# A gated attention layer on one core: queries, keys and gates projected transposed over 512 tokens, and an earlier layer norm

## The chip, the cores and the metric

The kernel runs on one core of a Trainium2 chip. The core has TensorE (PE in the rows: matmuls, and PEld: its weight loads), VectorE (DVE), ScalarE (ACT), GpSimd (POOL), and SyncE (SP), which issues the DMA transfers here. Each engine takes its instructions in order; engines wait for each other through semaphores. The metric is the device time of one execution in microseconds, as the median of several runs.

## The reference, cut to what matters

A layer norm over x (2048 tokens, 1024 features) is followed by one projection, whose 7592 columns are cut into queries, keys, values and gates of three branches. Branch A attends to the 256 keys that an index score selects, B is a differential attention with 4 heads of two softmaxes, C attends to 256 memory tokens. Each branch output is multiplied by silu of its gate, projected, weighted with a sigmoid gate, and the sum is projected and normalized.

```python
h = _layer_norm(x, ln_in_g, ln_in_b)
proj = h @ w_in[l]
(a_q, a_k, a_v, a_gate, i_q, i_k, i_w, b_q, b_k, b_v, b_gate,
 c_q, c_gate, m_gate) = _split_cols(proj, IN_SPLITS)
a_q = _partial_rope(a_q.reshape(bsz, seq, A_HEADS, A_HEAD_DIM), pos)
...
o_a = _dsa_attention(a_q, a_k, a_v, i_q, i_k, i_w).reshape(bsz, seq, A_WIDTH)
y_a = (o_a * jax.nn.silu(a_gate)) @ w_proj_a[l]
...
y_b = (o_b.reshape(bsz, seq, B_WIDTH) * jax.nn.silu(b_gate)) @ w_proj_b[l]
y_c = (o_c.reshape(bsz, seq, C_WIDTH) * jax.nn.silu(c_gate)) @ w_proj_c[l]
g = jax.nn.sigmoid(m_gate.reshape(bsz, seq, N_BRANCH, D_MODEL))
merged = g[:, :, 0] * y_a + g[:, :, 1] * y_b + g[:, :, 2] * y_c
h = _layer_norm(DEEPNORM_ALPHA * h + merged @ w_out[l], ln_g[l], ln_b[l])
```

`_partial_rope` rotates the first 16 of a head's 64 features (two halves of 8) by an angle that depends on the token.

## The kernel before, in words

Every fp32 matrix product is done with operands split into a high and a low part (`split`, L62 to L69: a copy, and a subtraction that leaves the rest), and three matmuls (`mm3`, L71 to L74). Tokens come in 16 blocks of 128; `hP` holds the split, transposed h for pairs of blocks, 256 tokens, and half of the blocks (8) is resident at a time.

The program has four stages. (1) For each half of the tokens: the layer norm and transposition (`prologue`, L187), the jobs `dense_ai` (queries of A in two jobs `aq`, then the index job `dense_ai01`: A's key and value, index queries, keys and weights), the search for the 256 best keys of each token (`topk_group`; VectorE and ScalarE count scores above a threshold bit by bit, L520, L529, L533), and `dense_b` (`bk`, `bv`, `bq`). For blocks 8 to 15 x is loaded and normalized only behind `dense_b(0)`. (2) B attention (from L647): logits `lg` (L623, L624), a copy to `P` with a running minimum (L633, L637), exp on ScalarE (L691), the two softmaxes combined (L697), transpositions `pt` (L703), their split `pr`, and the product with the values `ops` (L709), then a normalization (L712 to L724) and a store to `ob_d` (L725). (3) A attention (from L731) with the branches B and C projected beside it. (4) The branch A, the output projection `fz` and the last layer norm. The gate jobs `dense_g` (`cq`: C's queries, `sg`: silu gates, `tm`: sigmoid gates; 20 jobs per half) depend on h alone and can stand anywhere; they stand between other matmuls as filler.

A dense job (`dense`, L244) loads 256 columns of weights (`load_win`, `wr` raw, `w` split; the subtraction on GpSimd, the copy on ScalarE early on and on GpSimd later) and runs over 4 pairs of blocks into the PSUM tile `dps`. For `aq`, `bk`, `bv`, `bq` and the silu gates of A and B, h is the stationary operand and 256 weight columns move, so the output has tokens on partitions. For `cq`, `tm` and the gate of C the weights are stationary and 256 tokens move. The heads then go through `emit`: a copy to `do`, rope on GpSimd (L133 to L136), and `heads_out` (L212): a split of each 128-token block into `dt` on VectorE, four transpositions on TensorE (L223, into `dpt` or `psT`), a copy to `de` on ScalarE, and a store to DRAM. B and A attention load heads from DRAM again (`kg`, `bq`, `KA`, `aq`).

The order of the instructions on each engine is not written by hand: a list scheduler with a model of durations takes them from the program's order and its priorities (`tc.high_priority` raises those of `emit`), and each engine then runs its list in order. The pools with their numbers of buffers bound how far it can go ahead.

## Time and profile before

| | us |
|---|---|
| median of 3 runs | 2969.26 |
| lowest and highest run | 2966.13 and 2979.38 |
| the profiled execution's span | 2965.9 |
| TensorE busy in it | 2830.5 |
| VectorE busy | 2279.2 |
| ScalarE busy | 1442.6 |
| GpSimd busy | 983.2 |

The span of the profiled execution is what the rows below add up to. A busy time is the union of an engine's instructions; TensorE's matmuls overlap in the pipeline, so that a duration of one is longer than the distance between two starts. "Idle before" is the time in which an engine had nothing, and behind the arrow stands what released it.

### The profile page before, as it was taken

Reading aid. Unit: us, or ns where it says so; the run is one execution under the profiler, and the core shown is the slowest. Engines: PE = TensorE matmul, PEld = TensorE weight load, DVE = VectorE, ACT = ScalarE, POOL = GpSimd, SP = SyncE. Lnnn points to the kernel's source line nnn. Section 1 sums busy time; section 2 is a strip of 40 time slices with the busy share of each in tenths; the row PEclk is TensorE's granted clock in tenths of the full one; section 3 lists DMA queues with packets and bytes.
Section 4 is the critical chain, followed back from the end, with each engine's and each line's share of the span. In section 5 each row is a group of like instructions: output and inputs, shape, how many; then the busy total and the mean of one; then the engine's idle time right before and its main releaser. Section 6 shows DMA issues by size and latency. Waiting matters only on the chain. (4 is left out here: it accounts for less than half of the span.)

```text
span 2965.9 us, 57460 instructions
## 1 busy us (share of the span) xinstructions
PE 2830.5 (95%) x21616; PEld 2715.7 (92%) x21616; DVE 2279.2 (77%) x5309; ACT 1442.6 (49%) x2806; POOL 983.2 (33%) x1064
## 2 busy tenths in 40 slices
PE   7979998999999998999999999999999999988998
PEld 6979998999999998999999999988999999978887
DVE  6499988999899998676667766658787777776655
ACT  4345673677266772333344334446566556544100
POOL 6663547242522236323324222302222222200221
PEclk9999999999999999999999999999999999999999
DMA  6554434433232234624234242273433333256532
GB/s 208 171 191 138 159 113 156 133 119 114 94 101 76 82 93 147 201 73 140 89 118 142 77 128 80 75 242 110 133 114 119 102 113 102 86 172 224 172 131 79
DMA packets 320949, 379.47 MB, mean 128 GB/s; under 512 B 26400, under 2 KB 236832, under 8 KB 320160
## 3 DMA queue, kind: packets, MB, share of 16 engines
q1 hardware_dynamic: 320672, 375.80, 40.2%
q8 instruction: 171, 2.80, 0.4%
q14 instruction: 106, 0.87, 0.1%
HBM read 236.02 MB, written 139.69 MB: 127 GB/s over the span
## 5 line engine op out<-in xcount | busy, mean ns | idle before, releaser
L72 PE MATMUL dps<-hP,w 128*128 128x256 f32 x2048 | 582.6, 284 | 15.1 <-DVE do L69 9.9
L74 PE MATMUL dps<-hP,w 128*128 128x256 f32 x2048 | 581.7, 284 | 0.0
L73 PE MATMUL dps<-hP,w 128*128 128x256 f32 x2048 | 581.2, 284 | 0.0
L72 PE MATMUL dps<-w,hP 128*128 128x256 f32 (+1 forms) x1664 | 491.1, 296 | 12.5 <-POOL w L64 3.1
L73 PE MATMUL dps<-w,hP 128*128 128x256 f32 (+1 forms) x1664 | 490.0, 295 | 0.0
L74 PE MATMUL dps<-w,hP 128*128 128x256 f32 (+1 forms) x1664 | 487.9, 294 | 0.0
L72 PEld LDWEIGHTS dps<-hP,w 128*128 128x128 f32 x2048 | 392.6, 192 | 21.6 <-DVE do L69 10.7
L74 PEld LDWEIGHTS dps<-hP,w 128*128 128x128 f32 x2048 | 392.5, 192 | 4.4 <-POOL w L69 0.3
L73 PEld LDWEIGHTS dps<-hP,w 128*128 128x128 f32 x2048 | 392.7, 192 | 3.6
L533 ACT ACTIVATE ja<-sall,thr 128x1280 bf16<-128x1280 f32 (+4 forms) x224 | 302.2, 1349 | 122.6 <-DVE thr L529 107.1
L64 POOL TENSOR_SCALAR w<-wr 128x1024 fp32r<-128x1024 f32 x120 | 135.5, 1129 | 629.5 <-PE dps L74 404.9
L72 PEld LDWEIGHTS dps<-w,hP 128*128 128x128 f32 x1664 | 324.0, 195 | 16.8 <-issue 4.3
L69 POOL TENSOR_TENSOR w<-wr,w 128x1024 fp32r<-128x1024 f32 (+1 forms) x128 | 332.1, 2595 | 15.0 <-ACT w L66 6.9
L520 DVE TENSOR_SCALAR_CACHE_REDUCE jd<-sall,thr 128x1408 bf16<-128x1408 f32 (+6 forms) x231 | 330.9, 1433 | 5.9
L73 PEld LDWEIGHTS dps<-w,hP 128*128 128x128 f32 x1664 | 324.3, 195 | 1.8
L74 PEld LDWEIGHTS dps<-w,hP 128*128 128x128 f32 x1664 | 323.8, 195 | 2.2
L691 ACT ACTIVATE P<-P,nm 128x128 f32<-128x128 f32 (+15 forms) x128 | 154.1, 1204 | 197.8 <-DVE nm L690 187.5
L626 DVE CUSTOM_DVE_ANT_0 AP<-lg,bias 128x512 f32<-128x512 f32 (+3 forms) x304 | 181.9, 619 | 68.4 <-PE lg L624 25.1
L66 ACT CAST apr<-apt 128x512 fp32r<-128x512 f32 (+1 forms) x288 | 158.4, 563 | 141.7 <-PE apt L777 108.4
L633 DVE TENSOR_SCALAR_CACHE_REDUCE P<-lg 128x512 f32<-128x512 f32 (+3 forms) x288 | 170.4, 596 | 72.3 <-PE lg L624 71.2
L493 DVE SCALAR_TENSOR_TENSOR sall<-ir,iw,sall 128x512 f32<-128x512 f32 (+3 forms) x266 | 217.1, 865 | 8.9 <-ACT ir L489 8.0
L782 PE MATMUL aops<-apr,VA 128*128 128x256 f32 x1088 | 206.7, 297 | 16.8 <-DVE apr L69 6.7
(249 smaller groups left out, 7109.2 us busy)
## 6 DMA issues: line engine op xcount, KB each, us to landing
wr<-in_w_in_dram SPq DMA_DIRECT2D x112, 512.0 KB, 3.9
tm_d<-do SPq DMA_DIRECT2D x96, 256.0 KB, 2.1
bq<-qb_d SPq DMA_DIRECT2D x128, 128.0 KB, 3.1
aq<-qa_d SPq DMA_DIRECT2D x128, 128.0 KB, 3.1
yt<-tm_d SPq DMA_DIRECT2D x64, 256.0 KB, 3.6
sg_d<-do SPq DMA_DIRECT2D x48, 256.0 KB, 2.1
ys<-sg_d SPq DMA_DIRECT2D x48, 256.0 KB, 3.1
facc<-mg_d SPq DMA_DIRECT2D x48, 256.0 KB, 4.1
```

The source lines that it names most:

```text
L66: A.copy(H, src)
L69: el.tensor_tensor(L, src, H.bitcast(F32), op=ALU.subtract)
L72: PE.matmul(ps, lH, rH, start=start, stop=False)
L73: PE.matmul(ps, lH, rL, start=False, stop=False)
L74: PE.matmul(ps, lL, rH, start=False, stop=stop)
L493: V.scalar_tensor_tensor(s[:, c0:c0 + cn], r[:, :cn], iw[:, h:h + 1], s[:, c0:c0 + cn], op0=ALU.mult, op1=ALU.add)
L520: V.tensor_scalar(jd[:, :L], sc[b], t.bitcast(F32)[:, i:i + 1], None, op0=op, op1=ALU.add, accum_out=dst[:, i:i + 1])
L533: A.activation(ja[:, :L], sc[b], AF.Sign, bias=thr.bitcast(F32)[:, i:i + 1], scale=-1.0, accum_out=cnt[:, i:i + 1])
L626: V.tensor_tensor_reduce(P[:, c0:c0 + cn], ps[:, :cn], bias[:, c0:c0 + cn], scale=-0.125, scalar=-LOW, op0=ALU.add, op1=ALU.min, accum_out ...
L633: V.tensor_scalar(P[:, c0:c0 + n0], ps[:, :n0], -0.125, None, op0=ALU.mult, op1=ALU.min, accum_out=mx[:, col, nch:nch + 1])
L691: A.activation(p[:, :L], p[:, :L], AF.Exp, bias=nm[:, c:c + 1], scale=-1.0, accum_out=sm[:, c:c + 1])
L782: PE.matmul(o_ps.rearrange("p a d -> p (a d)"), VA[:, k0 + i], pr[:, a, i].rearrange("p e q -> p (e q)"), start=(k0 + i == 0 and a == 0), ...
```

## The change

All dense jobs except `bv` and the index job now have weights as the stationary operand and 512 tokens as the moving one, in `hQ` tiles of four blocks (the very first `aq` job still goes by 256). For `aq`, `bq`, `bk` the columns of a job's weights are put in another order while they are split (four strips of 32 columns, that hold the 8 features of a rope half for 4 heads, and then 128), so that rope on the transposed tile is three operations on 64 partitions, with a table `rope_t` that is loaded for each tile; the split of the result is on GpSimd, and nothing is transposed afterwards. `bv`'s split goes to GpSimd behind a copy on ScalarE. The silu gates of A and B are stored transposed, and `gated` multiplies after the transposition of the attention output instead of before. The layer norm of blocks 8 to 15 comes right behind `dense_ai(0)`; its result is stored to `h_d` and loaded again by `prologue` as `hx`. The input pool `xp` has 5 buffers instead of 8. The blocks of the second half's top-k groups are [8, 9, 14, 15] and [10, 11, 12, 13]. DRAM tiles hold 512 tokens. Over the program there are 4896 matmuls of 512 columns and 960 of 256 in place of 10752 of 256 into `dps`, 144 transpositions at the old L223 in place of 528, and 32 casts and 32 subtractions into `dt` in place of 128 each.

```diff
+        if len(src.shape) > len(H.shape):
+            H, L = (x.rearrange("p k (h d) -> p k h d", d=src.shape[-1]) for x in (H, L))
...
-    qa_d = [[dram(f"qa_d{j}_{p}", [4, 128, 256]) for p in range(NP)] for j in range(2)]
+    qa_d = [dram(f"qa_d{q}", [8, 128, 512]) for q in range(NQ)]
...
+            hQ[b // 4] = hTp.tile([128, 2, KT, 512], F32R, name=f"hQ{b // 4}", tag=f"hQ{b // 4 % 2}")
...
-    xp = pool("xp", 8, side="right")
+    xp = pool("xp", 5, side="right")
...
+    def normalize(b):
         xt = xin[b]
         mu, rs = norm_stats(p1, xt)
-        if b < 8:
-            nb = p1.tile([128, 1], F32, name="nb")
-            G.tensor_scalar(nb, mu, rs, -1.0, op0=ALU.mult, op1=ALU.mult)
-            A.activation(xt, xt, AF.Identity, bias=nb, scale=rs)
-        else:
-            V.tensor_scalar(xt, xt, mu, rs, op0=ALU.subtract, op1=ALU.mult)
+        nb = p1.tile([128, 1], F32, name="nb")
+        G.tensor_scalar(nb, mu, rs, -1.0, op0=ALU.mult, op1=ALU.mult)
+        A.activation(xt, xt, AF.Identity, bias=nb, scale=rs)
         (V if b < GV else G).tensor_tensor(xt, xt, gin, op=ALU.mult)
         V.tensor_tensor(xt, xt, bin_, op=ALU.add)
         SP.dma_start(h_d[b], xt)
+
+    def prologue(b, banks):
+        if b < 8:
+            normalize(b)
+            xt = xin[b]
+        else:
+            xt = dp.tile([128, D], F32, name="hx", bufs=3)
+            SP.dma_start(xt, h_d[b])
         to_hT(hT_tile(b), xt, banks)
...
+            H, L = (w[:, a, 4 * i:4 * i + 4, :n] for a in range(2))
+            if not heads:
+                split(H, L, raw, eh, el)
+                continue
+            rh = raw.rearrange("p k (h d) -> p k h d", d=64)
+            for u in range(4):
+                o = slice(32 * u, 32 * u + 32)
+                split(H[:, :, o], L[:, :, o], rh[:, :, :, 8 * u:8 * u + 8], eh, el)
+            split(H[:, :, 128:256], L[:, :, 128:256], rh[:, :, :, 32:64], eh, el)
...
+    def dense(kind, half, cols, idx, w=None, step=512):
         n = sum(c for _, c in cols)
         if w is None:
-            w = load_win(cols, A if early[0] else G)
-        for p in range(4 * half, 4 * half + 4):
-            ps = dqs.tile([128, 2, 256], F32, name="dps")
-            for i in range(2):
-                if kind in ("cq", "tm") or (kind == "sg" and idx[0] == 2):
-                    c = slice(i * 128, (i + 1) * 128)
-                    h = hP[p]
+            w = load_win(cols, A if early[0] else G, heads=kind in ("aq", "bq", "bk"))
+        if kind == "bv":
+            for p in range(4 * half, 4 * half + 4):
+                ps = dqs.tile([128, 2, 256], F32, name="dps")
+                for i in range(2):
+                    h = hT[2 * p + i]
                     for k in range(KT):
-                        mm3(ps[:, i], w[:, 0, k, c], w[:, 1, k, c], h[:, 0, k], h[:, 1, k], k == 0, k == KT - 1)
-                    continue
-                h = hT[2 * p + i]
-                for k in range(KT):
-                    mm3(ps[:, i, :n], h[:, 0, k], h[:, 1, k], w[:, 0, k, :n], w[:, 1, k, :n], k == 0, k == KT - 1)
+                        mm3(ps[:, i, :n], h[:, 0, k], h[:, 1, k], w[:, 0, k, :n], w[:, 1, k, :n], k == 0, k == KT - 1)
+                with tc.high_priority():
+                    emit(kind, idx, p, ps, n)
+            return
+        for g in range(2):
+            def col(a, k):
+                return w[:, a, k, 128 * g:128 * g + 128]
+            for q in range(2 * half, 2 * half + 2):
+                ps = dqs.tile([128, 512], F32, name="dps")
+                for c0 in range(0, 512, step):
+                    c = slice(c0, c0 + step)
+                    for k in range(KT):
+                        mm3(ps[:, c], col(0, k), col(1, k), hQ[q][:, 0, k, c], hQ[q][:, 1, k, c], k == 0, k == KT - 1)
+                with tc.high_priority():
+                    emit_t(kind, idx, g, q, ps)
+
+    def emit_t(kind, idx, g, q, ps):
+        if kind in ("sg", "tm"):
+            r, j = idx
+            o = dw.tile([128, 512], F32, name="do", bufs=3)
             with tc.high_priority():
-                emit(kind, idx, p, ps, n)
+                A.activation(o, ps, AF.Tanh, scale=0.5)
+                if kind == "sg":
+                    V.scalar_tensor_tensor(o, o, 1.0, ps, op0=ALU.add, op1=ALU.mult)
+            SP.dma_start((sg_d if kind == "sg" else tm_d)[r][q][:, 2 * j + g], o)
+            return
+        if kind == "cq":
+            e = [dw.tile([128, 512], F32R, name="do", bufs=3) for _ in range(2)]
+            with tc.high_priority():
+                split(e[0], e[1], ps, A, V)
+            for a in range(2):
+                SP.dma_start(cq_d[q][:, 2 * idx + g, a], e[a].bitcast(F32))
+            return
+        e = dp.tile([128, 2, 512], F32R, name="de")
+        dst = {"aq": qa_d, "bq": qb_d, "bk": kb_d}[kind][q].rearrange("h (a d) t -> h a d t", a=2)[4 * idx:4 * idx + 4]
+        if g:
+            o = dw.tile([128, 512], F32, name="do", bufs=3)
+            with tc.high_priority():
+                A.copy(o, ps)
+            split(e[:, 0], e[:, 1], o, G, G)
+            for a in range(2):
+                SP.dma_start(dst[:, a, 32:64], e.bitcast(F32)[:, a])
+            return
+        o = dw.tile([128, 512], F32, name="do", bufs=3)
+        sw = dp.tile([64, 512], F32, name="rsw", bufs=1)
+        with tc.high_priority():
+            A.copy(o, ps)
+            A.copy(sw[0:32], ps[32:64])
+            A.copy(sw[32:64], ps[0:32])
+        rq = dp.tile([64, 2, 512], F32, name="rq", bufs=1)
+        for i in range(2):
+            src = rope_t[i, :, :, 512 * q:512 * q + 512]
+            SP.dma_start(rq[32 * i:32 * i + 32], src[None].to_broadcast([4, 8, 2, 512]))
+        last_rope[0] = G.tensor_tensor(sw, sw, rq[:, 1], op=ALU.mult).ins
+        G.tensor_tensor(o[0:64], o[0:64], rq[:, 0], op=ALU.mult)
+        G.tensor_tensor(o[0:64], o[0:64], sw, op=ALU.add)
+        split(e[:, 0], e[:, 1], o, G, G)
+        for a in range(2):
+            for u in range(4):
+                SP.dma_start(dst[:, a, 8 * u:8 * u + 8], e.bitcast(F32)[32 * u:32 * u + 32, a])
...
         if kind == "bv":
             v = dp.tile([128, 2, 2, 2, 128], F32R, name="de")
+            o = dw.tile([128, 2, 256], F32, name="do", bufs=3)
             with tc.high_priority():
-                for i in range(2):
-                    pv = ps[:, i].rearrange("p (h d) -> p h d", d=128)
-                    split(v[:, :, i, 0], v[:, :, i, 1], pv, A, V)
+                A.copy(o, ps)
+            for i in range(2):
+                split(v[:, :, i, 0], v[:, :, i, 1], o[:, i].rearrange("p (h d) -> p h d", d=128), G, G)
...
+            dense("aq", half, [(C_AQ + 256 * j, 256)], j, W0 if first else None, 256 if first else 512)
...
+    for b in range(8, NB):
+        load_x(b, xp)
+        normalize(b)
...
+    topk_group([8, 9, 14, 15])
+    topk_group([10, 11, 12, 13])
...
+    def gated(pool, psp, pname, o, s, r, b, oT):
         t = slice(128 * (b % 2), 128 * (b % 2) + 128)
-        SP.dma_start(s, sg_d[r][b // 2][b % 2])
-        eng.tensor_tensor(o, o, s, op=ALU.mult)
+        SP.dma_start(s, sg_d[r][b // 4][:, :, 128 * (b % 4):128 * (b % 4) + 128])
         ps = psp.tile([128, 4, 128], F32, name=pname, bufs=2 if pname == "cps" else 1)
         for c in range(4):
             PE.transpose(ps[:, c], o[:, c * 128:(c + 1) * 128], idf)
         with tc.high_priority():
-            A.activation(oT[:, 0, :, t], ps, AF.Copy, scale=0.5)
-            V.scalar_tensor_tensor(oT[:, 1, :, t], ps, 0.5, oT[:, 0, :, t].bitcast(F32), op0=ALU.mult, op1=ALU.subtract)
+            V.scalar_tensor_tensor(s, ps, 0.5, s, op0=ALU.mult, op1=ALU.mult)
+            A.copy(oT[:, 0, :, t], s)
+            G.tensor_tensor(oT[:, 1, :, t], s, oT[:, 0, :, t].bitcast(F32), op=ALU.subtract)
```

The lists of the engines change with it. TensorE, the end of B attention, before (`lg<-KA` are A's first logits, `dps` a gate job):

```order
L72 MATMUL dps<-hP_25620,w 128x256
L73 MATMUL dps<-hP_25620,w 128x256
L623 MATMUL lg<-KA_15284,aq 128x512 x2
L74 MATMUL dps<-hP_25620,w 128x256
L72 MATMUL dps<-hP_25620,w 128x256
...
L624 MATMUL lg<-KA_15284,aq 128x512 x2
L73 MATMUL dps<-hP_25620,w 128x256
```

A's first logits stand among the last gate matmuls. TensorE, the last gate matmul, after (`pt`, `lg<-kg`, `ops` are B's):

```order
L76 MATMUL dps<-hQ_22199,w 128x512
L77 MATMUL dps<-hQ_22199,w 128x512
L745 MATMUL pt<-idf,P 128x128 x8
L667 MATMUL lg<-kg,bq 128x512
L668 MATMUL lg<-kg,bq 128x512
...
L751 MATMUL ops<-vg,pr 128x256
...
L751 MATMUL ops<-vg,pr 128x256 x8
L745 MATMUL pt<-idf,P 128x128 x3
L751 MATMUL ops<-vg,pr 128x256 x7
```

Behind this there are no more `dps` in the list: 434 of 1088 `ops`, 217 of 544 `pt` and 170 of 448 `lg` of 512 columns are still to come in B, and then A. TensorE, the end of B, after:

```order
L745 MATMUL pt<-idf,P 128x128 x2
L751 MATMUL ops<-vg,pr 128x256 x4
L745 MATMUL pt<-idf,P 128x128
L751 MATMUL ops<-vg,pr 128x256 x2
L667 MATMUL lg<-KA_13800,aq 128x512 x2
L668 MATMUL lg<-KA_13800,aq 128x512 x2
```

The last `ops` of B are followed directly by A's logits.

GpSimd in the first index job, before (`w_1207` is the second piece of its weights, `rt` and `do` rope):

```order
L69 TENSOR_TENSOR w_1207<-wr,w_1207 128x4x256
L133 TENSOR_TENSOR rt<-do,rp 128x8x8
L134 TENSOR_TENSOR rt<-do,rp 128x8x8
L69 TENSOR_TENSOR w_1207<-wr,w_1207 128x4x168
L135 TENSOR_TENSOR do<-do,rp 128x8x16
L136 TENSOR_TENSOR do<-do,rt 128x8x16
L133 TENSOR_TENSOR rt<-do,rp 128x8x8
L134 TENSOR_TENSOR rt<-do,rp 128x8x8
L64 TENSOR_SCALAR w<-wr 128x1024
L135 TENSOR_TENSOR do<-do,rp 128x8x16
L69 TENSOR_TENSOR w<-wr,w 128x1024
```

The piece is split among short operations. GpSimd at the same piece, after (`w_977`; `xt` the normalization of blocks 8 to 15, `de`, `rsw` and `do<-do,rq` query tiles):

```order
L325 TENSOR_TENSOR do<-do,rsw 64x512
L72 TENSOR_TENSOR de<-do,de 128x512
L117 TENSOR_TENSOR rs<-rs,mhalf 128x1
L196 TENSOR_TENSOR xt<-xt,gin 128x1024
L324 TENSOR_TENSOR do<-do,rq 64x512
L67 TENSOR_SCALAR de<-do 128x512
L72 TENSOR_TENSOR w_977<-wr,w_977 128x4x256
L196 TENSOR_TENSOR xt<-xt,gin 128x1024
L194 TENSOR_SCALAR nb<-mv,rs 128x1
L323 TENSOR_TENSOR rsw<-rsw,rq 64x512
L72 TENSOR_TENSOR de<-do,de 128x512
L72 TENSOR_TENSOR w_977<-wr,w_977 128x4x168
```

In front of it stand query tiles and multiplications of the normalization, which were further down.

## Rows read from the trace of the kernel before

**Rows 1.** The page, part 1: busy us, share, instructions of each engine.

```profile
PE 2830.5 (95%) x21616; PEld 2715.7 (92%) x21616; DVE 2279.2 (77%) x5309; ACT 1442.6 (49%) x2806; POOL 983.2 (33%) x1064
```

**Rows 2.** By stage: length; busy PE, PEld, DVE, ACT, POOL (count); clock; DMA; GB/s.

```profile
0.00:395.50 395.50, 346.81 (x2704) 339.66 (x2705) 321.81 (x633) 205.38 (x420) 226.09 (x283) 0.96 0.52 171
395.50:1190.00 794.50, 757.14 (x6127) 749.36 (x6127) 725.81 (x1149) 466.22 (x754) 325.02 (x249) 0.98 0.36 112
1190.00:1923.00 733.00, 726.20 (x5655) 703.33 (x5654) 501.91 (x1697) 290.44 (x550) 227.21 (x321) 1.00 0.36 112
1923.00:1955.70 32.70, 32.70 (x276) 32.70 (x276) 10.40 (x41) 6.16 (x17) 9.37 (x22) 1.00 0.47 146
1955.70:2739.80 784.10, 749.27 (x5743) 706.02 (x5741) 590.41 (x1603) 453.58 (x1033) 145.74 (x144) 0.99 0.45 136
2739.80:2965.90 226.10, 218.40 (x1120) 184.61 (x1120) 128.89 (x188) 20.86 (x35) 49.76 (x47) 0.98 0.38 132
```

**Rows 3.** Timeline of PE: start us, duration us, engine, line, op, tiles, shape, count.

```profile
1899.94 0.48 PE L623 MATMUL lg<-kg,bq 128*128 128x512 f32 x1
1900.25 0.39 PE L624 MATMUL lg<-kg,bq 128*128 128x512 f32 x1
1900.48 0.28 PE L74 MATMUL dps<-hP,w 128*128 128x256 f32 x1
1900.60 0.28 PE L72 MATMUL dps<-hP,w 128*128 128x256 f32 x1
```

**Rows 4.** Groups of PE by line and shape: count, busy us, mean ns, idle before.

```profile
L709 PE MATMUL ops<-vg,pr 128*128 128x256 f32 x1088 | 166.3, 283 | 0.2 <-ACT pr L66 0.2
...
L623 PE MATMUL lg<-kg,bq 128*128 128x512 f32 x224 | 93.0, 415 | 2.0 <-DVE kp L722 0.8 <-DMA kg<-kb_d 0.7 <-DVE P L633 0.4
...
L703 PE MATMUL pt<-idf,P 128*128 128x128 f32 x544 | 78.2, 272 | 0.6 <-DVE P L697 0.6
```

**Rows 5.** Waits of PE, 0 to 1190 us: us in total, times, longest.

```profile
PE psT L223 <- DVE dt L69: 13.3, 8, 6.1
PE dpt L223 <- DVE dt L69: 12.3, 8, 3.8
```

**Rows 6.** Timeline of PE in the index job, same columns as rows 3.

```profile
151.53 0.45 PE L223 MATMUL dpt<-idr,dt 128*128 128x128 f32 x4
158.04 0.72 PE L223 MATMUL psT<-idr,dt 128*128 128x128 f32 x4 [6.05 <-DVE dt L69]
```

**Rows 7.** Groups of POOL by line and shape, whole program.

```profile
L69 POOL TENSOR_TENSOR w<-wr,w 128x1024 fp32r<-128x1024 f32 x124 | 325.5, 2625 | 12.8 <-ACT w L66 4.9
L64 POOL TENSOR_SCALAR w<-wr 128x1024 fp32r<-128x1024 f32 x118 | 133.6, 1133 | 625.0 <-PE dps L74 404.9 <-DMA wr<-in_w_in_dram 204.8 <-DMA wr<-in_w_mem_kv_dram 10.6
...
L196 POOL TENSOR_TENSOR xt<-xt,gin 128x1024 f32<-128x1024 f32 x13 | 34.4, 2649 | 9.5 <-DVE xt L195 5.4 <-PE dps L74 3.4 <-DVE pre L538 0.6
```

**Rows 8.** Timeline of POOL: second piece of the index job's weights.

```profile
83.86 1.65 POOL L69 TENSOR_TENSOR w<-wr,w 128x672 fp32r<-128x672 f32 x1 [1.75 <-ACT w L66]
```

**Rows 9.** Groups of DVE by line and shape, 0 to 1190 us.

```profile
L69 DVE TENSOR_TENSOR dt<-do,dt 128x256 fp32r<-128x256 f32 x128 | 76.1, 620 | 0.2
...
L68 DVE CAST dt<-do 128x256 fp32r<-128x256 f32 x128 | 50.0, 415 | 42.8 <-POOL do L136 31.9 <-PE dpt L223 8.7 <-PE psT L223 1.4
```

**Rows 10.** Line 529 (top-k threshold): count, ns least/median/most, first and last start.

```profile
L529 DVE SCALAR_TENSOR_TENSOR thr<-pre,flip x93: 116/165/2398, 251.3 to 1096.1; 128x4 int32<-128x4 int32 x62, 128x6 int32<-128x6 int32 x31
```

**Rows 11.** Timeline of the SP queue at the end of B attention.

```profile
1943.08 0.38 SPq L732 DMA_DIRECT2D KA<-ka_d  x1
...
1953.62 0.80 SPq L749 DMA_DIRECT2D bias<-bias_d  x1
```

**Rows 12.** Timeline of DVE there; in brackets idle before and its releaser.

```profile
1942.29 0.35 DVE L724 SCALAR_TENSOR_TENSOR o<-o,rsb,g 128x128 f32<-128x128 f32 x1 [1.34 <-POOL rsb L723]
1958.87 0.69 DVE L626 CUSTOM_DVE_ANT_0 AP<-lg,bias 128x512 f32<-128x512 f32 x1 [16.23 <-DMA bias<-bias_d]
```

125 lines of the change are left out of this document (46 added, 79 removed).

## Prediction

> **What bounds the kernel now.** I read the totals first, then the windows by stage, then TensorE's timeline for the spacing of matmuls, then the waits, and last the order of both kernels. TensorE is busy 95% of the span [rows 1], but this is a mean of two situations [rows 2]. Up to 1190 us (prologue, the top-k search, most of the dense jobs) TensorE is busy 347 of 395.5 and 757 of 794.5 us, at a mean granted clock of 0.96 and 0.98, beside a VectorE that is busy 81% and then 91%: 86 us idle, and more lost in stretches at the lower of the two clock levels. From 1190 to 1955.7 us (B attention) TensorE is busy 759 of 766 us, VectorE 67%. The reason is in the listing: dense gate matmuls stand between the attention's matmuls to the end of B and beyond it, so TensorE always has work while a softmax is unfinished.
>
> I count TensorE's work by start-to-start times. A 512-column matmul takes 0.23 us, one of 256 columns 0.12 [rows 3] and a 128x128 transposition of fp32 about 0.11; the fp32r transpositions of L223 about 0.07 [rows 6]. The durations in the groups [rows 4] overlap and are not used for sums. Over the whole program the instructions of before make 2736 us by these spacings, of which 1054 stand ahead of B's first logits.
>
> **The change part by part.**
>
> *512 moving columns.* 9792 matmuls of 256 columns become 4896 of 512: 2 x 0.120 - 0.232 = 0.008 us each, 37 us in all. It is small because the columns streamed stay the same.
>
> *No head transpositions.* 384 L223 transpositions go, at about 0.07 us: 26 us of TensorE, all before 1190. With them go VectorE's splits of head tiles: 96 casts and 96 subtractions, 96 x (0.415 + 0.620) = 99 us [rows 9], in a stretch where VectorE is 91% busy. TensorE waits 25.6 us for these splits now [rows 5]. About two thirds of it belong to the index job, which keeps its form (the 6 us wait in rows 6 is such a one), so I let 9 us go, and some 5 us of the slow clock that follows such waits (the granted clock's mean of 0.96 in [rows 2]).
>
> *GpSimd's new work.* 24 head tiles take three rope operations and two pairs of splits on 512 columns; half of a 1024-column one is 1.3 us for a subtraction and 0.57 for a scale [rows 7], so 3 x 1.3 + 2 x 1.9 = 7.7 us each, 185 in all, less 96 us of old rope, plus about 31 us of the v splits: 120 us more, on 551 of 1190 [rows 2]. A heads job takes 15.4 + 7.5 us (its weights) and 1 to 3 us for the cut strips, 24 to 26 us, beside 96 matmuls x 0.232 = 22.3 us of TensorE. So GpSimd is level with TensorE in these jobs and catches up in v and index jobs; on the sum I cost it at nothing, from -5 (rope freed earlier) to +35 us.
>
> *Layer norm of blocks 8 to 15 early.* In GpSimd's order their gamma multiplications (2.65 us each) now stand ahead of the split of the second piece of the index job's weights, seven of them with the rope of the query tiles. Before, the last of this piece ended at 85.5 us [rows 8], behind short operations, just as TensorE came to the index job at 86. Adding up GpSimd's queue by rows 7, it reaches this piece at 103 to 112 us, TensorE at 85 to 88: I take 17 us of wait, bounds 0 (the second piece is only needed from the second half of the first tile on) and 25. The eight tiles of h are now stored and loaded again, 8 loads of 512 KB more on SP's queue while DMA is busy 52% and then 36% [rows 2]: +3 us, from 0.
>
> Ahead of the second index job, then: work 297 instead of 319 us (the new order has a few jobs later), losses 77 + 17 - 9 - 5 + 3 = 83: it starts at 380 instead of 395.5. From there to B's first logits the work is 733 (735 before), and the loss was 60 us. With 99 us less on VectorE, spread over both stretches, I let a third of it go, to 37: B begins at 380 + 770 = **1150 us instead of 1190**, bounds 1130 and 1185.
>
> *B attention.* This is where the order decides. In the changed order the last dense matmul stands before 434 of the 1088 output matmuls, 217 of the 544 transpositions and 170 of the 448 logit matmuls of 512 columns of B; before, 91 dense matmuls even stood behind the last of B. The dense work ran out early because the scheduler placed it so, and A's logits stand directly behind B's last output matmul. Up to that last dense matmul: 1659 x 0.232 = 385 us, logits 81, transpositions 36, outputs 78, memory projection 23, in all 603 us; times 733/719, as that stretch ran on its work before, 615 us. The rest of B, 40% of it, runs without filler. TensorE's part of it is 170 x 0.232 + 7 + 217 x 0.109 + 434 x 0.12 = 122 us. VectorE's: it was busy 512 us in 1190 to 1955.7 [rows 2], 22 of it on dense outputs, so 490 on B; 38% (the share of the logits) is 186 us, 40% is 196. VectorE is then the bound. In the stretch where it is the busiest it reaches 91%, so 186 / 0.91 = 203 us; bounds 186 (no gap) and 225 (the exp on ScalarE and the normalization's chain, each of which VectorE waits for, stand open). Then A's start: its keys are issued at 1943.08, its bias at 1953.62 [rows 11], and VectorE's first A operation comes at 1958.87 after 16.2 us for that bias [rows 12]. This was covered by dense matmuls; now it is open: 16 us, and 3 of drain. So from the last dense matmul to A's first logits 222 us, bounds 205 and 245. A begins at 1150 + 615 + 222 = 1987 instead of 1956.
>
> *A attention and the rest.* 1010 us before [rows 2], less 91 x 0.12 = 11 us of dense matmuls that ended there. Gating on transposed tiles moves 64 multiplications of 0.7 us or more between engines and leaves TensorE's transpositions as they are; w loads change only their tile. I take 1000, bounds 993 and 1012.
>
> Sum: 380 + 770 + 615 + 222 + 1000 = 2987 us of span against 2965.9, so +21. The profiled span is 3.4 us below the median of the runs: **2990 us**.
>
> **A rule on wide matmuls.** Two logits of 512 columns stand 0.23 us apart [rows 3]. The Trainium skill ("TensorE: Matmul & The Clock Gate", section "Back-to-back issue gap") states a sustained 131 ns for N=512; by that the 4896 wide matmuls would save some 530 us. The logits' rows at 512 columns disagree, so this rival, at about 2500 us, has 1 in 100.
>
> **The rivals.**
>
> (a) *The head of the program gives back its idle.* VectorE falls to about 85% before 1190, the index weights come in time, and TensorE waits for nothing much: B begins at 1095 to 1110, and the tail runs at its lower bound of 205. Then 1102 + 615 + 205 + 998 + 3 = about 2920 us. For it: nearly all idle there is behind VectorE or starts with it. Against: the startup (22 us), the index job's own waits and the top-k chain stay. Chance 0.20.
>
> (b) *Level.* No wait for the index weights and a tail at VectorE's sum: B at 1135, tail 210, rest 1000: 1135 + 615 + 210 + 1000 + 3 = 2963. Chance 0.25.
>
> (c) *GpSimd becomes the bound of the first 1190 us.* Its busy share rises from 46 to about 57%, and 24 to 26 us per heads job beside 22.3 is over the line from the point where a heads job has no slack ahead of it. Also, VectorE's short operations stretch beside it: L529 takes 116 ns at least, 165 in the median, and 2398 at most [rows 10], about as long as one GpSimd subtraction [rows 7]. At 6 heads jobs in a row x 3 us and some 15 longer operations of 1.5 us in the top-k chain, +40 us: 3030. The Trainium skill ("SBUF — State Buffer", section "Who interferes with whom") names the cause, a port pair that VectorE and GpSimd share under an exclusive lock; L529's spread agrees. Chance 0.15.
>
> (d) *Wide matmuls save nothing*, or B's order on the chip has its filler late after all, so that the change doesn't do what it says: the first gives +30 us on my sum, 3020, the second -80, 2910. Chance 0.03 together.
>
> **How the numbers follow.** My case has 0.36 (2970 to 3015 by its bounds), the rest stands above, 0.01 for the rule on N. About 0.5%, 15 us, is what a measurement of this kernel can tell from no change: faster is below 2954, slower above 2984. Slower gets most of my case (0.33), (c) and half of (d), 0.50; faster (a), the other half and the rule, 0.22; same (b) and the low end of my case, 0.28. The range 2915 to 3040 leaves out the far half of (a) and the ends of (c).
>
> **What the new profile would show.** Right: TensorE near 99% busy in B until about 1765 us, then some 60% with VectorE near 90% until about 1975; a hole of 10 to 16 us before A's first logits; a GpSimd wait of TensorE near 90 us; dense matmuls 0.23 us apart. Wrong: TensorE over 85% in the last 200 us of B (the tail's bound is not VectorE), B's first logits before 1110, or GpSimd as the releaser of more than 40 us of TensorE's idle.

## The result

| | before | after |
|---|---|---|
| median of the runs shown together, us | 2971.74 (4 runs) | 3128.85 (4 runs) |
| the profiled execution's span, us | 2965.9 | 3128.0 |

The ratio is 1.0528, 95% interval 1.0506 to 1.0549: the change makes the kernel slower by 5.3%, and its time lies 89 us above the top of the predicted range. The first page line of after stands against rows 1: TensorE is busy nearly as long as before, in a longer span, VectorE hardly less, and GpSimd 222 us more.

```profile
PE 2823.1 (90%) x16336; PEld 2463.6 (79%) x16336; DVE 2256.4 (72%) x5045; ACT 1429.1 (46%) x2750; POOL 1205.0 (39%) x1304
```

By stage, the windows of after, cut at the same places of the program as rows 2 (start of the first and of the second index job, B's first logits, the last gate matmul, A's first logits, the output projection). The columns are those of rows 2. (Before, B's first logits stand at 1193.8 us, a little behind the cut at 1190 in rows 2; the table further down cuts at the logits.)

```profile
0.00:116.30 116.30, 66.79 (x353) 59.15 (x354) 62.77 (x93) 44.70 (x71) 97.48 (x108) 0.84 0.69 224
116.30:453.10 336.80, 277.45 (x1441) 239.55 (x1440) 249.48 (x441) 176.51 (x371) 225.72 (x305) 0.91 0.44 143
453.10:1320.40 867.30, 765.92 (x3648) 642.79 (x3646) 720.62 (x1010) 438.85 (x684) 437.46 (x349) 0.94 0.35 113
1320.40:1924.00 603.60, 600.96 (x3251) 517.05 (x3250) 348.85 (x1138) 203.45 (x393) 197.01 (x245) 1.00 0.36 112
1924.00:2115.60 191.60, 150.84 (x884) 124.05 (x882) 161.42 (x591) 93.31 (x169) 31.74 (x92) 0.88 0.28 87
2115.60:2903.90 788.30, 744.72 (x5660) 698.09 (x5660) 587.07 (x1593) 452.66 (x1032) 163.27 (x158) 0.98 0.44 132
2903.90:3128.00 224.10, 216.42 (x1108) 182.95 (x1108) 126.23 (x181) 19.68 (x33) 52.36 (x49) 0.98 0.37 127
```

A busy time doesn't tell what a stage lost, because it holds stretched matmuls at the lower clock. So I sum for each stage the work that TensorE did, matmul by matmul, at the distances between two starts in the kernel before (0.231, 0.192, 0.1195 us for 512, 424 and 256 columns, 0.109 and 0.07 for transpositions of fp32 and fp32r; the first and third are those of rows 3), and call the rest of the stage's length lost: idle, or the slow clock behind it. The wide gate matmuls of after stand 0.227 us apart, so up to 20 us that this table counts as their work could be counted as lost.

| stage, us | before: length, work, lost | after: length, work, lost |
|---|---|---|
| to the first index job | 86, 56, 30 | 116, 52, 64 |
| to the second index job | 309, 262, 47 | 337, 244, 93 |
| to B's first logits | 798, 735, 64 | 867, 730, 137 |
| B to the last gate matmul | 762, 751, 11 (all of B) | 604, 601, 3 |
| from there to A's first logits | | 192, 122, 69 |
| A and the branches | 784, 714, 70 | 788, 704, 84 |
| output projection | 226, 214, 12 | 224, 213, 11 |
| sum | 2966, 2732, 234 | 3128, 2666, 462 |

TensorE does 66 us less work, about as forecast, and loses 228 us more: 153 ahead of B, 61 in B, 14 in A. The prediction had the end of B about right, and the stage before it wrong by 170 us. The end of B first, from TensorE's timeline and SyncE's (`aq` are A's queries):

```profile
1923.97 0.39 PE L77 MATMUL dps<-hQ,w 128*128 128x512 f32 x1
1924.20 1.03 PE L745 MATMUL pt<-idf,P 128*128 128x128 f32 x8
...
2101.11 1.24 PE L751 MATMUL ops<-vg,pr 128*128 128x256 f32 x2 [0.41 <-ACT pr L69]
2115.58 1.19 PE L667 MATMUL lg<-KA,aq 128*128 128x512 f32 x2 [13.23 <-DMA aq<-qa_d]
```

```profile
2106.37 0.38 SPq L774 DMA_DIRECT2D KA<-ka_d  x1
2106.80 0.42 SPq L776 DMA_DIRECT2D VA<-va_d  x1
2107.32 7.41 SPq L787 DMA_DIRECT2D aq<-qa_d  x8
```

Behind the last gate matmul TensorE needs 192 us for 122 us of work, at a mean granted clock of 0.88; in the last 13.2 us of them it stands with no cover until A's queries have landed. Ahead of B TensorE is idle for 210 us, before for 86; half of the 210 (105 us, before 19) ends with ScalarE, 70 with VectorE (62) and 34 with GpSimd (4). No single wait holds more than a quarter of it (the five largest, 0 to 1320 us, against rows 5; `dps` is a dense job's PSUM tile, `rsw` and `do` copies of one, `w` the split weights, `hQ` and `xt` the tokens' h and its source):

```profile
PE dps L75 <- ACT rsw L318: 47.3, 13, 12.1
PE dps L75 <- POOL w L67: 26.8, 3, 14.9
PE psT L183 <- DVE xt L197: 25.2, 4, 15.6
PE dps L75 <- ACT hQ L69: 18.7, 4, 10.9
PE dps L75 <- DVE do L72: 15.5, 5, 7.5
```

One of them in full. TensorE's longest wait in the dense jobs is for ScalarE's copy of a query tile out of PSUM; the copies stand in ScalarE's queue behind the cast of a weight piece, which waited 14.63 us for its load; the load was issued at 88.55, behind query stores on SyncE, one of which waited 3.2 us for GpSimd, and was there 6.9 us later (timelines of TensorE, ScalarE, SyncE):

```profile
97.93 0.79 PE L75 MATMUL dps<-hQ,w 128*128 128x512 f32 x1 [12.05 <-ACT rsw L318]
```

```profile
95.46 0.75 ACT L69 CAST w<-wr 128x672 fp32r<-128x672 f32 x1 [14.63 <-DMA wr<-in_w_in_dram]
96.12 0.58 ACT L316 COPY do<-dps 128x512 f32<-128x512 f32 x1
96.72 0.58 ACT L317 COPY rsw<-dps 32x512 f32<-32x512 f32 x1
97.31 0.57 ACT L318 COPY rsw<-dps 32x512 f32<-32x512 f32 x1
```

```profile
85.40 3.04 SPq L329 DMA_DIRECT2D qa_d<-de  x2
88.55 0.46 SPq L345 DMA_DIRECT2D wr<-in_w_in_dram  x1
```

Four queues, TensorE's, ScalarE's, SyncE's and GpSimd's, stand in that one wait.

### The profile page after: what moved, and what is told of

Same layout as the page of the kernel before. It is cut to its first block, busy times and chain, and to the rows that moved or that the text cites. A ratio compares the mean times of both kernels' runs of the same rounds, so it can differ in the third digit from the quotient of the medians.

```text
span 3128.0 us, 47100 instructions
## 1 busy us (share of the span) xinstructions
PE 2823.1 (90%) x16336; PEld 2463.6 (79%) x16336; DVE 2256.4 (72%) x5045; ACT 1429.1 (46%) x2750; POOL 1205.0 (39%) x1304
## 4 chain that ended last, share of the span: by engine, by line
PE 54%; DVE 17%; DMA 9%; POOL 7%; issue 7%; ACT 5%; SPq 1%; POOLq 0%; DVEq 0%; ACTq 0%
PE dps L75 7%; PE dps L76 6%; PE dps L77 6%; DVE jd L565 4%; PE ops L751 3%; PE aops L824 3%; PE lg L667 3%; PE lg L668 3%; PE apt L819 3%; ACT ja L578 3%; PE yps L75 3%; PE yps L76 3%; PE yps L77 3%; PE fz L75 2%; PE fz L76 2%
## 5 line engine op out<-in xcount | busy, mean ns | idle before, releaser
L75 PE MATMUL dps<-hQ,w 128*128 128x512 f32 (+1 forms) x1696 | 682.1, 402 | 107.2 <-ACT rsw L318 47.3
L76 PE MATMUL dps<-hQ,w 128*128 128x512 f32 (+1 forms) x1696 | 675.9, 398 | 3.9 <-DVE hQ L72 3.9
L77 PE MATMUL dps<-hQ,w 128*128 128x512 f32 (+1 forms) x1696 | 673.2, 397 | 0.0
L75 PEld LDWEIGHTS dps<-hQ,w 128*128 128x128 f32 x1696 | 331.4, 195 | 187.4 <-ACT rsw L318 52.6
L76 PEld LDWEIGHTS dps<-hQ,w 128*128 128x128 f32 x1696 | 331.8, 196 | 68.1 <-DVE hQ L72 5.0
L77 PEld LDWEIGHTS dps<-hQ,w 128*128 128x128 f32 x1696 | 330.9, 195 | 65.3
L67 POOL TENSOR_SCALAR w<-wr 128x1024 fp32r<-128x1024 f32 (+2 forms) x200 | 161.5, 820 | 549.9 <-PE dps L77 318.5
L72 POOL TENSOR_TENSOR w<-wr,w 128x1024 fp32r<-128x1024 f32 (+2 forms) x224 | 347.5, 1566 | 11.6 <-ACT w L69 4.9
L565 DVE TENSOR_SCALAR_CACHE_REDUCE jd<-sall,thr 128x1920 bf16<-128x1920 f32 (+6 forms) x231 | 331.2, 1434 | 7.4
L538 DVE SCALAR_TENSOR_TENSOR sall<-ir,iw,sall 128x512 f32<-128x512 f32 (+3 forms) x266 | 246.9, 985 | 81.1 <-ACT ir L534 79.8
L75 PE MATMUL yps<-yoT,whQ 128*128 128x256 f32 x768 | 221.4, 289 | 4.8 <-ACT yoT L873 3.6
L72 DVE TENSOR_TENSOR apr<-apt,apr 128x512 fp32r<-128x512 f32 (+1 forms) x288 | 185.7, 656 | 48.3 <-ACT apr L69 46.8
L76 PE MATMUL yps<-yoT,whQ 128*128 128x256 f32 x768 | 219.6, 286 | 0.2 <-POOL yoT L874 0.2
L77 PE MATMUL yps<-yoT,whQ 128*128 128x256 f32 x768 | 218.6, 285 | 0.0
L534 ACT ACTIVATE ir<-ips 128x512 f32<-128x512 f32 (+3 forms) x304 | 149.8, 551 | 130.3 <-PE ips L529 93.5
L811 ACT ACTIVATE AP<-AP,anm 128x1024 f32<-128x1024 f32 (+7 forms) x192 | 172.1, 900 | 62.5 <-DVE anm L808 58.9
```

Source lines behind the costliest of these rows:

```text
L67: G.tensor_scalar(H, src, 1.0, 1.0, op0=ALU.mult, op1=ALU.mult)
L72: el.tensor_tensor(L, src, H.bitcast(F32), op=ALU.subtract)
L75: PE.matmul(ps, lH, rH, start=start, stop=False)
L76: PE.matmul(ps, lH, rL, start=False, stop=False)
L77: PE.matmul(ps, lL, rH, start=False, stop=stop)
L538: V.scalar_tensor_tensor(s[:, c0:c0 + cn], r[:, :cn], iw[:, h:h + 1], s[:, c0:c0 + cn], op0=ALU.mult, op1=ALU.add)
```

## The experiments

Theories: F, the width of 512 spoils the list of instructions (gate work is used up too early); heads, the transposed query and key tiles cost more than they save, through GpSimd (P), SyncE's queue (S) or the PSUM tile that ScalarE holds (R); L, the early layer norm delays the start. All times are medians beside runs of the kernel before on the same chip (its medians go from 2963 to 2972 us); "lost" is counted as above.

One thing limits all that follows: with every edit the scheduler makes new lists for all engines. Ahead of B, GpSimd's order in the traces parts from that of the change at the 57th of 761 instructions in e16 and e15, at the 65th in e2 and at the 73rd in e14. So a time shows what an edit does together with the order that came with it, and an edit that doesn't help has not fully cleared the engine it relieves. Of the edits to the changed kernel only e10 leaves the order ahead of B nearly as it was.

### One part undone

**e1, layer norm late again** (`load_x(b, p1)` and the normalization back in the loop behind `dense_b(0)`).

```diff
-    for b in range(8, NB):
-        load_x(b, xp)
-        normalize(b)
...
     for b in range(8, NB):
+        load_x(b, p1)
         with tc.high_priority():
             prologue(b, [(tq, "ips", 4)])
```

> The changed kernel with one part undone: the layer norm of blocks 8 to 15 stands again behind dense_b(0), on VectorE, with x loaded there. Theory L (the early layer norm holds GpSimd, the x loads and the DMA queue in the first 170 us, and that delay of 43 us at the end of the first index job is carried through): the first index job starts at about 95 instead of 116 us, B's first logits at about 1280 instead of 1320, the time is 3085 to 3095 us. Theory P (GpSimd's head tiles hold the PSUM tiles of the dense jobs all through the first stage): the start is a little earlier, but the loss comes back job by job, and the time stays over 3110 us.

Measured 3177.0 us, ratio 1.072: 48 us slower than the change. The index job starts at 106 instead of 116 us, but between the two index jobs 146 us are lost instead of 93. The time is in theory P's range. Theory L falls: with the orders that the scheduler makes, this kernel is faster with the early layer norm.

**e3, old heads.** `aq`, `bq`, `bk` go through the old branch (256 columns moving, `rope_apply`, `heads_out`); the rest of the change stays.

> The changed kernel with the heads (aq, bq, bk) as before: h stationary, 256 columns moving, rope on small tiles, splits on VectorE and transpositions on TensorE; gates transposed over 512 tokens, v split on GpSimd and early layer norm stay. Theory P: most of the 127 us that the first stage lost come back, B's first logits at 1200 to 1225 us, the time 3010 to 3040 (B's second part still without filler). Theory L: 43 us of the start stay and are not made up for, B at 1240 to 1260, the time 3055 to 3080. If neither heads nor layer norm matters but the width of 512 and the hQ tiles of four blocks, over 3100.

Measured 3049.9 us, ratio 1.029. Ahead of B 161 us are lost (34.7 + 48.4 + 77.5) instead of 294: the transposed heads cost 133 us of TensorE's time there, and save 29 us of work there, 35 in all. B still loses 79 us (72 in the change), and the time is 10 us above theory P's range. With the first index job at 90.4 and the second at 401.8 us, the start is nearly that of before.

**e6, gates alone.** Heads, v, layer norm, `xp` and top-k groups as before; gates 512 wide, transposed, gating behind the transposition.

> The gate jobs alone: 512 moving tokens for cq, sg and tm, gating after the transposition and hQ tiles of four blocks, with heads, v, layer norm, input buffers and top-k groups as before. Both theories: the first stage is like that of before, B's first logits at 1185 to 1215 us. In its order 488 of 1088 output matmuls of B come behind the last gate matmul (434 in the changed kernel), so by the account of the tail (VectorE's 40 to 45% of B at 0.9, and an open start of A) B takes 70 to 90 us more of TensorE's time than it needs, against 29 us of matmuls saved: 3000 to 3030 us. If the tail doesn't cost, 2940 to 2960.

Measured 3035.3 us, ratio 1.024. To the third group's scores everything stands where it stood before (they begin at 811.1, before at 810.8). Then the scores take 161 us instead of 104, and B's end has no gate work: 75 us are lost between the last gate matmul (1810.1) and A's logits (2023.0). Both theories had B begin by 1215; it begins at 1259, and the time is 5 us above the range.

**e4, 256 columns everywhere.**

```diff
-    def dense(kind, half, cols, idx, w=None, step=512):
+    def dense(kind, half, cols, idx, w=None, step=256):
```

> The changed kernel with 256 moving columns in all dense jobs (two accumulations per PSUM tile instead of one), everything else as it is; TensorE has 37 us more to do. Theory F: the scheduler's list then has gate matmuls left to the end of B, the third group's scores are fed as before, and the time falls in spite of the 37 us, to 3060 to 3105. Rival W or P alone: the 37 us are added, 3145 to 3170.

Measured 3089.5 us, ratio 1.040: 39 us faster than the change and inside theory F's range, though TensorE has some 37 us more to do. B loses 13.5 us instead of 72; ahead of B the losses of the heads stay (269 instead of 294).

**e12 and e13, the same for e3 and for e6** (old heads, and gates alone, with 256 columns).

> The kernel e3 (old heads; transposed gates, early layer norm, v split on GpSimd, new top-k groups) with 256 moving columns in the gate jobs instead of 512. Theory F (the width of 512 spoils the scheduler's order): the third group's scores fall from 140 us to about 95, the tail of B has its gate work, B starts at 1160 to 1185, and the time is 2930 to 2965, faster than the kernel before by what the early layer norm brings. Rival W (512-token hQ tiles, transposed gates): 3030 to 3060 as e3 plus nothing.

> The kernel e6 (only the gates transposed and gating moved; all else as before) with 256 moving columns instead of 512. Theory F: the list of TensorE has again some 638 gate matmuls among the last group's scores and gate work to the end of B, now of the width it was planned with: the time is that of the kernel before, 2955 to 2980. Rival W: what e6 lost stays, 3020 to 3050.

Measured 3013.8 (1.016) and 2985.6 us (1.006). e13 lies 6 us above the range of theory F; e12 lies 49 us above it and below that of W: it loses 162 us ahead of B, as e3 does and some 20 more than the kernel before. So in three pairs the narrower matmuls are faster, by 36 (e3, e12), 50 (e6, e13) and 39 us. The list shows why. The gate instructions among the last group's scores (windows of that stretch with the tile `dps` alone; kernel before, e6, e13):

```profile
810.80:915.20 104.40, 94.48 (x637) 83.59 (x637) 3.38 (x5) 8.40 (x14) 1.00 0.28 88
```

```profile
811.10:972.00 160.90, 141.96 (x588) 108.02 (x587) 3.39 (x5) 14.90 (x25) 1.00 0.29 92
```

```profile
810.70:914.50 103.80, 94.69 (x638) 83.67 (x639) 4.07 (x6) 8.42 (x14) 1.00 0.27 84
```

637 of 256 columns before and 638 in e13, 588 of twice the width in e6: the scheduler puts in about as many instructions as before, and on the chip each takes twice as long. In the changed kernel the first quarter of B's output matmuls has 714 wide and 96 narrow ones beside it, where before there were 981 narrow, and the last quarter none (794 before).

### Where gate work is missing

**e21, mixed widths.** e6 with 256 columns in the second token half's gates (among the scores) and 512 in the first half's (in B).

> The gates-only kernel e6 with 256 moving columns in the gate jobs of the second token half (they stand among the last group's scores) and 512 in those of the first half (they stand in B attention). In the list, 638 narrow gate matmuls stand among the scores, as before, and B again has no gate work in its last 36%. Theory F, with the loss at the scores: the scores take 104 us again, B starts at 1190 to 1205, B takes 740 to 765 us as in e6, the time is 2960 to 2985. If the missing gate work at the end of B were a loss of its own (as the prediction had it): B takes 785 or more, the time is 2990 to 3010.

Measured 3046.0 us, ratio 1.027. The scores are fed as before and B starts at 1197.6 (before 1193.8), but B takes 825 us: 654 to the last gate matmul, 171 behind it. The windows:

```profile
1197.60:1851.50 653.90, 651.90 (x3514) 560.43 (x3513) 365.23 (x1201) 217.41 (x415) 210.07 (x263) 1.00 0.36 113
1851.50:2022.40 170.90, 132.14 (x788) 107.36 (x787) 144.85 (x536) 83.29 (x153) 25.01 (x82) 0.91 0.31 94
```

Against e13, which has its gate work to the end of B:

```profile
1195.50:1963.40 767.90, 762.14 (x5967) 741.16 (x5968) 522.71 (x1736) 297.06 (x565) 231.92 (x342) 1.00 0.36 112
```

The lower range of the expectation falls, and the time is 36 us above even the upper one. The prediction's own mechanism stands: the missing gate work at B's end is the loss (62 us lost there; 19 of TensorE's 24 us of idle end with VectorE, which is busy 85%, and the mean granted clock is 0.91). In e6 the same loss only looked like a late start of B: gate work that was done among the scores was missing later.

**e8, gates alone with an order forced on the list**, and **e10, the change with the same**: gate jobs from the eleventh on are queued behind the last score matmul, those of the first token half behind evenly spread transpositions of B.

```diff
+            if half and i >= 10:
+                after = last_ips[0]
+            elif not half and i >= 5:
+                after = marks[(i - 4) * len(marks) // 16]
...
+                with tc.issue_after(after):
+                    dense(kind, half, [(c0, 256)], idx)
```

> The gates-only kernel e6 with one edit in the order: the gate jobs of the second half from the eleventh on stand behind the last score matmul of the last top-k group, and those of the first half are spread over B attention, so that 283 wide gate matmuls stand among the last group's score matmuls where e6 has 587 (the kernel before has 637 of half the width), and the last eighth of B still has its share. Theory F (the scheduler puts about as many gate matmuls between waiting instructions as before, each is twice as long on the chip, so the scores that feed the top-k search come late and B's second half has no gate work left): the last group's scores take 100 to 115 us instead of 161, B's logits start at 1185 to 1215 us instead of 1259, the time is 2925 to 2965. Rival W (the 512-token tiles themselves cost it, through coarser PSUM tiles or hQ tiles of four blocks): 3000 to 3040, as e6.

> The changed kernel with the same edit in the order (gate jobs held back, spread over B). Theory F with theory P for the heads: the 136 us that the last group's scores take fall to 95 to 110, B starts at 1275 to 1295 instead of 1320, B takes its 760 us, the start of A is covered again, and the time is 3050 to 3095; what stays of the loss, some 90 us, is the heads'. If the heads' tiles are harmless once the order is mended: 2930 to 2970. If the order is not the cause: 3115 to 3140.

Measured 3070.6 (1.034) and 3168.2 us (1.067), each some 35 to 39 us slower than without, and above all the ranges expected. The scores get shorter, about as expected (119 us in e8, B at 1210.8; 92 us and 1257 in e10). But in e8 TensorE, with less gate work among the scores, loses 27 us there, where e6 loses none; ahead of B that makes 115 us lost instead of 83, which is all that e8 is slower by. And B gains nothing, though it has 369 to 387 wide gate matmuls in each of its last three quarters: it loses 52 us on its way (75 in e10) and 23 more at its end, where A's load stays uncovered, together about as much as e6 (77); in e10 B loses 26 us more than in the change. So presence of gate work is not enough; what the finer order in e13 has that these lack isn't settled.

### What carries the heads' loss

Each takes one suspect away from the changed kernel, in the order that the scheduler then makes.

**e2, the split of head tiles on ScalarE and VectorE.**

```diff
-            split(e[:, 0], e[:, 1], o, G, G)
+            split(e[:, 0], e[:, 1], o, A, V)
```

> The changed kernel with one edit: the split of the head tiles (48 copies and 48 subtractions of 512 columns, 91 us of GpSimd) on ScalarE and VectorE instead of GpSimd; rope stays on GpSimd. Theory P: TensorE's wait for the rsw copies (47 us) and for weights from GpSimd (34 us) falls by half or more, B's first logits come at 1250 to 1280 us instead of 1320, the time is 3060 to 3090. Theory L: nothing of the start changes, and the time stays within 15 us of 3129. If the top-k search on VectorE is what bounds the stage, VectorE's 35 us more make it 3140 to 3165.

Measured 3191.9 us, ratio 1.077: slower by 63, and above all three ranges. **e15, less on GpSimd**, without anyone else taking it over:

> The changed kernel with less work on GpSimd for the heads: one of the three rope operations and the subtraction of the low halves are left out, 24 x 1.3 + 48 x 1.25 = 90 us; the high half is stored twice, so that SyncE has the same transfers. Theory P: TensorE's idle in the first 800 us falls from 168 to 100 to 130 us, B starts at 1240 to 1280, the time is 3045 to 3090. Theory S: 3110 to 3135.

Measured 3177.3 us, ratio 1.071: slower by 48 and above both ranges, though GpSimd has less to do (busy 664 us ahead of B instead of 761) and TensorE's work is the same. Theory P's gain does not come: less load on GpSimd is not enough by itself. TensorE's waits in e15 have moved to weights and index queries:

```profile
PE dps L75 <- POOL w L67: 43.2, 3, 25.4
PE dps L75 <- ACT w L69: 28.6, 1, 28.6
PE ips L528 <- DMA qi<-qi_d: 28.2, 3, 18.8
```

**e7, head stores issued by GpSimd** (`G.dma_start` for the ten stores of a pair of tiles), and **e14, fewer transfers on SyncE**.

> The changed kernel with the ten stores of each pair of head tiles issued by GpSimd, which makes the tiles, instead of SyncE. Theory S (SyncE's queue is in order: 240 head stores wait there for GpSimd, and the loads of the next weights, of x and of the rope table wait behind them, and ScalarE's and GpSimd's queues wait for these): TensorE's idle in the first 800 us falls by 25 to 60 us, the time to 3065 to 3105. Theory P (GpSimd's own load): the issuing comes on top of it, 3130 to 3180.

> The changed kernel with less in SyncE's queue for the heads: the eight stores of the small strips of a head tile are two stores of the same bytes (in a wrong order of rows), and the rope table is loaded once instead of for every tile, so 190 transfers less; GpSimd's, ScalarE's and TensorE's work is unchanged. It leaves the right order of rows and the right rope table out. Theory S (SyncE's queue is what holds the loads of weights): TensorE's idle in the first 800 us falls from 168 to 110 to 140 us, B starts at 1250 to 1290, the time is 3055 to 3095. Theory P (GpSimd): 3110 to 3135.

Measured 3246.5 (1.093) and 3131.6 us (1.055). In e7, above both ranges, the 240 stores hold GpSimd's queue for some 0.6 us each, 149 us in all, and TensorE's waits for `rsw` go from 47 to 108 us. In e14, 190 transfers less on SyncE change nothing: their number is not what costs. Whether it matters what a store waits for in that queue is not tested by it.

**e16, PSUM free after one copy**, **e17, four `de` tiles** (paid for with one `hx`), **e18, both**.

```diff
-            A.copy(sw[0:32], ps[32:64])
-            A.copy(sw[32:64], ps[0:32])
+            A.copy(sw[0:32], o[32:64])
+            A.copy(sw[32:64], o[0:32])
```

> The changed kernel with one edit in the heads: ScalarE's two copies into rsw read the tile do instead of the PSUM tile, so that the PSUM tile is free after one copy (0.58 us) instead of three in a row (1.7 us), each of which can stand behind top-k work in ScalarE's queue. Theory R (TensorE waits in the heads because the PSUM tile is held by ScalarE's chain of copies): TensorE's 47 us of waits for the rsw copies fall below 15, its idle in the first 800 us falls from 168 to 120 to 145, the time to 3080 to 3110. If the wait only moves to the next thing that holds the chain (do, de or the weights): 3115 to 3135.

> The changed kernel with four buffers instead of two for the split head tiles de, and one instead of three for hx (the reloaded h), which pays for them. Theory D (GpSimd waits 65 us for stores of head tiles to free de, with the weights' splits behind it in its queue; the stores wait in SyncE's order): GpSimd's waits for these stores fall below 20 us, TensorE's idle in the first 800 us to 110 to 140, the time to 3070 to 3105. Otherwise 3120 to 3145, more by a few us for the single hx.

> Both edits, e16 and e17, together. If the heads' loss is a chain in which each queue waits for the next (PSUM tile, ScalarE, do, GpSimd, de, SyncE), both together give more than the sum of each: 3040 to 3080. If neither is the link: 3115 to 3140.

Measured 3131.9, 3202.6 and 3203.3 us. In e16 the 47 us of waits for `rsw` are gone, and have moved one link on, to the copy into `do` (TensorE's waits, 0 to 1320 us):

```profile
PE dps L75 <- ACT do L308: 26.6, 6, 9.0
PE psT L183 <- DVE xt L197: 24.8, 4, 15.6
PE dps L75 <- ACT do L316: 23.5, 9, 5.9
```

R's gain does not come: the place of the wait moves, the time stays. e17 and e18, above all their ranges, do not decide about `de`: with one `hx` TensorE waits 22 to 29 us for the reloaded h, and GpSimd's wait for weight loads grows (213 us in e17 against 124 in the change).

**e19, old heads for A's queries alone.**

> The changed kernel with A's queries alone as before (h stationary, transpositions on TensorE); B's queries and keys stay transposed. It tells where the heads cost: the aq jobs stand at the start, where the first top-k search waits for the index job behind them, and once more ahead of the second; bk and bq stand behind. If the cost goes by tiles (8 of 24 are aq's), a third of e3's 79 us comes back: 3095 to 3110. If the start is what is carried through: the first search begins at 255 to 265 us instead of 296, and the time is 3060 to 3085.

Measured 3096.6 us, ratio 1.044: 32 us faster than the change. Ahead of B 250 us are lost instead of 294: 44 for 8 of 24 tile pairs, where all 24 cost 133. That is 5.5 us a pair in both, as expected of a cost that goes by tiles and not by the place of the first ones.

### The early layer norm by itself

**e22**: e13 with the layer norm early.

> The kernel e13 (gates transposed at 256 columns, all else as before) with the early layer norm of blocks 8 to 15 added, alone. Against e13 (2986 us): if the early layer norm is a gain by itself, as undoing it in the changed kernel cost 48 us (e1), 2935 to 2965. If it only repays what the transposed heads' queues cost, and its GpSimd operations and loads delay the first top-k search: 2985 to 3010.

Measured 3002.4 us, ratio 1.012: 17 us slower than e13. B starts 13 us earlier, with 20 us less gate work done; that work stands in A's stage and in the output projection (1060 us from A on, against 1016). TensorE loses 23 us more than in e13: 7 ahead of B, 7 in B, 9 behind. Where TensorE is the bound to the end, an earlier start that leaves work undone gives nothing.

None of these kernels is faster than the one before.

## Why the prediction was wrong, step by step

**The sum's failing step** is "on the sum I cost it at nothing, from -5 ... to +35 us": GpSimd's new work in the heads. By e3 and the change, the transposed heads cost 133 us of TensorE's time ahead of B (294 lost against 161) and save 35 us of work in all. I compared GpSimd's throughput with TensorE's per job, 24 to 26 us beside 22.3, and took the rest for covered. The term behind it was also too small: GpSimd's busy time ahead of B rose by 207 us (554 to 761), not 120, mostly because the weights' splits with their cut strips took 47 us more over the program and the v splits 51 us, not 31. By these numbers a heads job takes, as an estimate, 28 us of GpSimd. But its load alone is not the cause either (e15). What the waits show in place of the cover is that a head tile now goes through ScalarE (three copies), GpSimd (five operations, in a queue with the weights' splits), SyncE (up to 12 transfers) and back to free `do`, `de` and PSUM, and that TensorE's idle ahead of B rose by 124 us, 87 of them ended by ScalarE. That the sum of these ways through queues is the cost fits the one wait followed above and the edits that only moved the waits; it is argued, not shown. Rival (c) had the direction and 40 us. Its releaser, GpSimd with over 40 us of TensorE's idle, is not what the waits show (34 us), and none of the prediction's three signs of being wrong appeared: it did not watch ScalarE. Which link would free the chain stays open: taken alone, and each in a new order, GpSimd's load (e15), SyncE's number of transfers (e14) and the PSUM tile (e16) do not; the `de` buffers were not tried without a cost elsewhere.

**VectorE's 99 us.** They went: `dt` has 48 casts and 48 subtractions in the groups of after against 144 each before (the index job's 16 of each counted in). But VectorE's busy time ahead of B fell only from 1048 to 1033 us, mostly because the same 266 score operations, and the same short top-k ones, took longer (groups of VectorE, 0 to 1325 us, before and after):

```profile
L493 DVE SCALAR_TENSOR_TENSOR sall<-ir,iw,sall 128x512 f32<-128x512 f32 (+3 forms) x266 | 217.1, 865 | 8.9 <-ACT ir L489 8.0
```

```profile
L538 DVE SCALAR_TENSOR_TENSOR sall<-ir,iw,sall 128x512 f32<-128x512 f32 (+3 forms) x266 | 246.9, 985 | 81.1 <-ACT ir L534 79.8
```

These, the first score operation and the three short ones of a search step, 589 operations in all, are busy for 335 us before, 346 in e3, 370 in e15 and 404 after, in the order of GpSimd's busy time ahead of B (554, 614, 664 and 761 us). In all twenty kernels here it goes broadly that way: summed operation by operation, they take 345 to 365 us where GpSimd is busy for up to 614 us ahead of B, 386 and 388 in the two at 664 and 666, and 402 to 430 above 700. The Trainium skill ("SBUF — State Buffer", section "Who interferes with whom") describes a port pair that VectorE and GpSimd share under an exclusive lock; these numbers agree with it, though no run here sets the two engines against each other alone. I had weighed it for (c) at 15 operations of 1.5 us; it took 69 us. And e15, where part of it comes back, is no faster, so it isn't by itself what bounds the stage.

**The weights of the first index job.** The piece was late (its split ended at 121.4 us), but TensorE came to this job only at 116.3 and waited 1.6 us in its first tile. The 12 us shown above stand ahead of the job, behind ScalarE's cast of an earlier piece and its load on SyncE, not behind GpSimd's split. A wait of the kind that I had forecast came in the second index job: 14.9 us at 475.6. To the first index job 34 us more are lost, where I had 17 and 3.

**From the second index job to B** I let the loss fall from 60 to 37; it rose to 137. With the heads as before (e3) it was 78: no idle was given back there either. So VectorE's 99 us were not what TensorE lacked there; what it was is not isolated.

**The end of B.** Right in its mechanism, which e21 against e13 shows apart, and right in TensorE's 122 us; mis-sized in VectorE's share: 161 us busy, not 186, so that the stretch took 192 us and not 222 (its lower bound was 205). Up to A's open start, in 178 us, VectorE is busy for 160, 90% where I had 91, so the occupancy was right. I had worked the share out of the count of logits still to come, 38%; of the operations that combine the two softmaxes (L739 after) 21 of 64 were to come, 33%. A's open start came about as forecast (13.2 us, forecast 16 and 3). To the last gate matmul B took 604 us, forecast 615.

**Width.** The saving per matmul is as worked out (0.227 to 0.231 us for 512 columns), 66 us of work with the transpositions against 63 in the steps. The sustained 131 ns of the Trainium skill ("TensorE: Matmul & The Clock Gate", section "Back-to-back issue gap") is not met here: the wide gate matmuls start 0.227 us apart in the median. What I left out is that the list doesn't follow the width: it has about as many instructions in a stretch, each twice as long. The order was there to read; I read its end in B, and not its scores, where the same count of gate matmuls stood.

**A and the branches** took 1012 us, forecast 1000.

## What to carry to other kernels

Where a scheduler fills gaps with independent matmuls, an edit that makes each of them longer also moves when they run out: count the filler in the new list stretch by stretch, in time and not in instructions, before a saving per matmul is believed. A transposition that leaves TensorE and VectorE and comes back as more steps through several in-order queues is not costed by the busy time of the engine that takes it over: here that looked covered, and TensorE lost 5.5 us a pair of tiles. Which measure would have told is not shown here. And on a kernel whose main engine is the bound to the end, an early start of one stage is worth only what it takes off that engine's idle time.

## What had not been expected of the hardware

Short VectorE operations next to a busier GpSimd: the comparison `bit` that ends a step of the top-k search (L537, L582 after) went from a mean of 435 to 635 ns in the same 96 operations, with a median of 164 and 167 ns and a longest of 2372 and 4631 ns. The longest has nearly doubled: before, it was shorter than one of GpSimd's subtractions of 1024 columns (2625 ns, [rows 7]), after, not much shorter than two. The threshold operation that the prediction watched [rows 10] did not follow: its 93 are busy for 37.9 us before and 37.6 after.
